# Two feed-forward blocks by seven-product block multiplication: C11 computed ahead for six pairs instead of four, and the last two products of each of their units moved behind the first two of the next unit

## The chip, the cores and the metric

The kernel runs on one core of a Trainium2 chip. The metric is the time that the device takes for one execution, in microseconds (us). An execution that the hardware profiler recorded has a time of its own, and its trace has a span, from the first to the last instruction.

A core has five engines that run side by side, each with a queue of its own that it works through in order: PE (TensorE, matrix multiplication into PSUM, with its weight loads shown as PEld), DVE (VectorE, elementwise), ACT (ScalarE, elementwise and functions), POOL (GpSimd) and SP (SyncE). Here POOL and SP mostly issue DMA transfers. An instruction that has to wait holds up everything behind it in its engine's queue.

## The reference, cut to what matters

One decoder layer over 1024 tokens of width 1024: a SwiGLU block, a mixer of two attention groups, and a second SwiGLU block. The hidden width D_FF is 2816.

```python
def _swiglu(x, g, w_gate, w_up, w_down):
    h = _rms(x, g)
    return (jax.nn.silu(h @ w_gate) * (h @ w_up)) @ w_down
...
x = x + FFN_RESID * _swiglu(x, ffn1_norm[l], ffn1_w_gate[l], ffn1_w_up[l], ffn1_w_down[l])
h = _rms(x, mix_norm[l])
...
x = x + o.astype(x.dtype) @ w_out[l]
x = x + FFN_RESID * _swiglu(x, ffn2_norm[l], ffn2_w_gate[l], ffn2_w_up[l], ffn2_w_down[l])
```

The change touches only how `h @ w_gate` and `h @ w_up` are ordered, in both blocks.

## The kernel before, in words

**Blocks and products.** `ffn` is called once for each SwiGLU block. The hidden width is 22 tiles of 128, taken as 11 pairs `c` (`NF // 2`). A pair has a gate and an up matrix, so there are 22 units, written here 0g, 0u, 1g and so on. In a unit the weights are four blocks M11, M12, M21, M22 (two hidden tiles by two halves of the features), the activations four blocks B11, B21 (first half of the tokens) and B12, B22 (second half), and the result four blocks C11, C12, C21, C22 of 128x512. The four are made with seven block products instead of eight. The operands on the weight side are M11, M12, M22 and S1 = M21 + M22, S2 = S1 - M11, S3 = M11 - M21, S4 = M12 - S2. On the activation side they are B11, B21, B22 and the sums T1 to T4.

- C11 = M11 B11 + M12 B21
- with U = M11 B11 + S2 T2: C22 = U + S3 T3 + S1 T1, C12 = U + S1 T1 + S4 B22, C21 = U + S3 T3 + M22 T4

**A product** (`product`, L357; `products`, L115) is 4 blocks of the contraction by 3 matmuls: each operand is split into a high and a low part (`split`, L99: ACT copies the high part at L101, DVE subtracts it from the source at L102), and high*high, high*low, low*high are accumulated (L122, L124, L126). So a product is 12 matmuls of 128x128 by 128x512, pinned in the order in which the program writes them. Other instructions are placed on their engines by a scheduler that follows the program's order closely.

**A unit's closing work.** `middle` (L572) takes two PSUM banks, Dk for S1 T1 and E for S3 T3, then a third, A, for S2 T2. DVE then forms `a` (U), and in two more additions C22: `a = kept + A` (L586) in the first pairs, `q = a + E` (L587), `q = q + Dk` (L588). `close` (L591) adds S4 B22 into the same bank Dk, so its first matmul must wait until L588 has read Dk. DVE forms C12 (L596). M22 T4 is added into E and DVE forms C21 (L600). `silu` (L604) runs on ACT on the gate's results, `finish` (L361) multiplies gate by up (L368, L373), stores the result to the DRAM tensor `act` and makes four more sums of it for the down projection (L385 to L388, stored at L389, L383, L390).

**The first pairs.** C11 needs only B11 and B21, so for the first FRONT = 4 pairs `front` (L394) computes M11 and M12 of two pairs at a time (16 products in all) before the rest. Meanwhile ACT and DVE make B22 and T1 to T4 from the second half of the tokens (`second_half`, L251, lines L264 to L280). The product M11 B11 is needed again in U: it is copied (L402), stored to the DRAM tensor `p1` (L404), and loaded back as `kept` (L579) in `middle`. C11 of gate times up goes to `act` through a small tile (L368, L369) and is loaded back later next to C22 (L376), and both leave with L377. All of these transfers are issued by POOL.

**The order around the change.** The list `order` (L291 to L302) gives the order in which weight operands are used. `prepare` makes them up to five products ahead, and `load_units` starts the load of a unit's raw weights (two tiles of 512 KB, L286, issued by SP) when the unit before it is made. The calls at L611 to L634 issue the products in the same order:

- pairs 0 to 3: S4 and M22 of the previous pair's up unit (`close_up`); S1, S3, S2 of g; S4, M22 of g; S1, S3, S2 of u
- pairs 4 to 10: M11, M12 of g (`start`, L558); S4, M22 of the previous up unit; S1, S3, S2 of g; M11, M12 of u; S4, M22 of g; S1, S3, S2 of u

In the first form S4 of a unit follows directly on S2 of the same unit. In the second form two products of another unit stand between them. After the pairs, `down` (L530) computes the down projection with matmuls at L518 to L520.

Of the kernel before, what the change touches and what calls it, by code (L numbers as in the profile page):

```python
# [18 lines left out]
P = 128  # L19
# [4 lines left out]
NF = DFF // P  # L24
# [22 lines left out]
CSTART = 0.5  # L47
EARLYH = 4
LEAD = 3
FRONT = 4  # L50
ESTEPS = 5
CEND = 4
MSTART = 6.5
# [8 lines left out]
def tile_layer(ctx: ExitStack, tc: tile.TileContext, x, g1n, mixn, g2n, wg1, wu1, wd1, wg2, wu2, wd2,  # L62
# [27 lines left out]
    def tmp(shape, dt=F32):  # L90
        return tpool.tile(shape, dt, tag="tmp", name=nm("tmp"))
# [131 lines left out]
    def ffn(rows_in, ys, gain, wg, wu, wd, act_d, xsrc, done, lead, aside=iter(())):  # L223
# [66 lines left out]
        PAIRS = range(NF // 2)  # L290
        order = [(c + i, m, w) for c in range(0, FRONT, 2) for w in ("M11", "M12") for i in range(2) for m in "gu"]  # L291
        for c in PAIRS:
            if c >= FRONT:
                order += [(c, "g", w) for w in ("M11", "M12")]
            if c > 0:
                order += [(c - 1, "u", w) for w in ("S4", "M22")]
            order += [(c, "g", w) for w in ("S1", "S3", "S2")]
            if c >= FRONT:
                order += [(c, "u", w) for w in ("M11", "M12")]
            order += [(c, "g", w) for w in ("S4", "M22")]  # L300
            order += [(c, "u", w) for w in ("S1", "S3", "S2")]
        order += [(NF // 2 - 1, "u", w) for w in ("S4", "M22")]  # L302
        units = [(True, c, m) for c in range(FRONT) for m in "gu"] + [(False, c, m) for c in PAIRS for m in "gu"]
        raws, sums_, ready = {}, {}, {}
# [8 lines left out]
        def make(c, nme, which):  # L313
            front = c < FRONT and which in ("M11", "M12")
            u = (front, c, nme)
            load_units(units.index(u) + (3 if front else 2))
            f1, f2 = raws[u][0], raws[u][-1]
            m = {"M11": f1[:, :512], "M12": f1[:, 512:], "M21": f2[:, :512], "M22": f2[:, 512:]}
            need = {"S1": ("M21", "M22", ALU.add), "S2": ("S1", "M11", ALU.subtract),
                    "S3": ("M11", "M21", ALU.subtract), "S4": ("M12", "S2", ALU.subtract)}  # L320
            if which in need:

                a_, b_, op = need[which]
                if which == "S1":
                    sums_["S1"] = tmp([P, 512])
                s1 = sums_["S1"]
                src = {"S1": s1, "S3": m["M21"], "S2": s1, "S4": m["M12"]}[which]
                nc.vector.tensor_tensor(src, s1 if a_ == "S1" else m[a_], s1 if b_ == "S2" else m[b_], op=op)  # L328
            else:
                src = m[which]  # L330
            s = slot([P, 2, 512], F32R)
            lows.append(split(s[:, 0, :], s[:, 1, :], src))
            ready[(c, nme, which)] = (s[:, 0, :], s[:, 1, :])
            if which == "M22" or (front and which == "M12"):
                del raws[u]
# [13 lines left out]
        def product(pt, c, nme, which, blk, first=True, ahead=AHEAD):  # L349
            assert order[used[0]] == (c, nme, which)  # L350
            prepare(ahead + 1)
            used[0] += 1
            w = ready.pop((c, nme, which))
            products(pt, [(cut(w, k * P, (k + 1) * P), blk.hi_lo(k)) for k in range(4)], first,
                     tc.keep_in_program_order)
# [3 lines left out]
        def finish(f, th, gate, up):  # L359
# [5 lines left out]
            key = "diagonal" if j == th else "other"  # L365
            if c < FRONT and j == th == 0:
                early = tmp([P, 512])
# [193 lines left out]
        def start(c, nme):  # L561

            A, Bk = ps(), ps()
            product(A, c, nme, "M11", B11)
            product(Bk, c, nme, "M12", B21)
            q = tmp([P, 512])
            nc.scalar.activation(q, A, AF.Copy)
            with behind_operands():
                nc.vector.tensor_tensor(q, q, Bk, op=ALU.add)  # L569
            return A, q  # L570

        def middle(c, nme, A):  # L572

            Dk, E = ps(), ps()
            product(Dk, c, nme, "S1", T1)
            product(E, c, nme, "S3", T3)
            if c < FRONT:
                A, kept = ps(), tmp([P, 512])
                nc.gpsimd.dma_start(kept, p1_d[c, :, "gu".index(nme), :])  # L579
            product(A, c, nme, "S2", T2, first=c < FRONT)  # L580
            a, q = tmp([P, 512]), tmp([P, 512])
            if c >= FRONT:
                nc.scalar.activation(a, A, AF.Copy)  # L583
            with behind_operands():
                if c < FRONT:
                    nc.vector.tensor_tensor(a, kept, A, op=ALU.add)  # L586
                nc.vector.tensor_tensor(q, a, E, op=ALU.add)  # L587
                nc.vector.tensor_tensor(q, q, Dk, op=ALU.add)  # L588
            return Dk, E, a, q

        def close(c, nme, Dk, E, a, between):  # L591

            product(Dk, c, nme, "S4", B22, first=False)
            q = tmp([P, 512])
            with behind_operands():
                nc.vector.tensor_tensor(q, a, Dk, op=ALU.add)  # L596
            between(q)
            product(E, c, nme, "M22", T4, first=False)
            with behind_operands():
                nc.vector.tensor_tensor(a, a, E, op=ALU.add)  # L600
            return q, a

        def silu(q):
            nc.scalar.activation(q, q, AF.Silu)  # L604

        def close_up(c, Dk, E, a, g12, g21):
            _, q = close(c, "u", Dk, E, a, lambda q: finish(2 * c, 1, g12, q))
            finish(2 * c + 1, 0, g21, q)

        late = None  # L610
        for c in PAIRS:  # L611
            if c in (4, 6):
                next(aside, None)
            A = Au = None
            if c >= FRONT:
                A, g11 = start(c, "g")
                silu(g11)
            if late:
                close_up(*late)
            Dk, E, a, g22 = middle(c, "g", A)  # L620
            silu(g22)
            if c >= FRONT:
                Au, u11 = start(c, "u")
                finish(2 * c, 0, g11, u11)
            if c == NF // 2 - 1:
                B11.t = B21.t = None
                for _ in range(2):
                    load_down(*loads.pop(0))
            g12, g21 = close(c, "g", Dk, E, a, silu)
            silu(g21)  # L630
            if c == KD - 1:
                fetch(2)
                for _ in range(PRELOAD - 2):
                    load_down(*loads.pop(0))  # L634
            Du, Eu, au, u22 = middle(c, "u", Au)
            finish(2 * c + 1, 1, g22, u22)
            late = (c, Du, Eu, au, g12, g21)
# [648 lines left out]
    order = [(h, 7 - j if h == DH + MH - 1 else j) for h in range(DH + MH) for j in range(8)]  # L1286
# [151 lines left out]
```

## Time and profile before

| | |
|---|---|
| median of 3 runs | 1913.47 us (1908.57 to 1915.0) |
| the profiled execution: its time | 1916.01 us |
| its span in the trace | 1914.2 us |
| mean granted TensorE clock of that execution | 0.983 |
| from the first down-projection matmul of the first block to its last | 474.1 to 696.1 us |
| the same in the second block | 1694.3 to 1908.9 us |

Times in the trace are counted from the span's start. A timeline row has the start, the duration, the engine, the line and operation, and in brackets how long the engine was idle before it and who ended that. A windows row has the length of a stretch, each engine's busy time with its number of instructions, the clock that TensorE was granted in the stretch (1.00 is full, 0.50 is half), the share of time that the DMA engines were busy, and GB/s. Names of buffers are `slot` (SBUF, 47 of 4 KB a partition), `tmp` (SBUF, 12 of 2 KB a partition) and `ps` (a PSUM bank, 8).

### The profile page before, as it was taken

To read this page: it belongs to the slowest core of one execution; us is meant where nothing else is said; L and a number is where in the kernel's file an instruction comes from. 1 tells how busy PE (TensorE), PEld (TensorE's weight loads), DVE (VectorE), ACT (ScalarE), POOL (GpSimd) and SP (SyncE) were. 2 spreads that over 40 slices of the span, in tenths; PEclk is the share of its full clock that TensorE was granted. 3 is DMA by queue.
4 is the path that set the end of the run, shared out by engine and by line. 5 is a ranking of instruction groups with operands and counts; after the bars stand their busy time and mean duration, and the time that the engine had idled before them with its cause. 6 is when DMAs were issued, how large, how long until landed. Compare 5 with 4: busy or idle time off the path is not lost.

```text
span 1914.2 us, 25117 instructions
## 1 busy us (share of the span) xinstructions
PE 1835.1 (96%) x9040; PEld 1548.7 (81%) x9040; DVE 1245.8 (65%) x2375; ACT 793.8 (41%) x1802; POOL 294.8 (15%) x508
## 2 busy tenths in 40 slices
PE   8888999999999999999998999997889999999998
PEld 6666888888888888889998988886678888888887
DVE  6857666665978273327888783467657665778671
ACT  7412323333445153235875672453223333334540
POOL 3011010000000022323354520211000000000000
PEclk9889999999999999999999999998999999999999
DMA  7334224324954241023311332333432332288422
GB/s 253 116 105 156 92 90 138 131 84 176 356 172 127 94 137 33 28 55 117 89 36 30 93 118 77 125 130 117 131 109 96 119 105 94 84 305 310 126 56 88
DMA packets 92326, 234.38 MB, mean 122 GB/s; under 512 B 12487, under 2 KB 18329, under 8 KB 92201
## 3 DMA queue, kind: packets, MB, share of 16 engines
q1 hardware_dynamic: 71592, 162.93, 26.3%
q0 software_dynamic: 20608, 69.85, 10.4%
q8 instruction: 71, 1.16, 0.2%
q14 instruction: 55, 0.44, 0.1%
HBM read 165.00 MB, written 63.53 MB: 119 GB/s over the span
## 4 chain that ended last, share of the span: by engine, by line
PE 85%; DVE 9%; ACT 2%; issue 2%; DMA 2%; POOL 1%; SPq 0%; DVEq 0%; ACTq 0%; POOLq 0%
PE ps L122 18%; PE ps L124 18%; PE ps L126 18%; PE ps L520 7%; PE ps L519 7%; PE ps L518 7%; DVE slot L102 2%; PE ps L847 2%; PE ps L873 1%; PE ps L821 1%; PE ps L912 1%; ACT slot L101 1%; PE ps L837 1%; PE ps L1035 1%; DMA slot<-in_wu_dram 1%
## 5 line engine op out<-in xcount | busy, mean ns | idle before, releaser
L122 PE MATMUL ps<-slot,slot 128*128 128x512 f32 (+3 forms) x1712 | 668.4, 391 | 48.7 <-DVE tmp L588 31.8
L124 PE MATMUL ps<-slot,slot 128*128 128x512 f32 (+3 forms) x1712 | 662.1, 387 | 3.6 <-DVE slot L102 3.6
L126 PE MATMUL ps<-slot,slot 128*128 128x512 f32 (+3 forms) x1712 | 661.5, 387 | 0.0
L122 PEld LDWEIGHTS ps<-slot,slot 128*128 128x128 f32 x1712 | 327.1, 191 | 118.5 <-issue 36.5
L124 PEld LDWEIGHTS ps<-slot,slot 128*128 128x128 f32 x1712 | 327.8, 191 | 66.6 <-DVE slot L102 4.4
L126 PEld LDWEIGHTS ps<-slot,slot 128*128 128x128 f32 x1712 | 326.7, 191 | 63.9
L102 DVE TENSOR_TENSOR slot<-slot,slot 128x512 fp32r<-128x512 f32 (+1 forms) x428 | 294.4, 704 | 36.1 <-ACT slot L101 33.9
L101 ACT ACTIVATE slot<-slot 128x512 fp32r<-128x512 f32 (+1 forms) x428 | 260.7, 638 | 104.3 <-PE ps L520 44.8
L101 ACT ACTIVATE slot<-tmp 128x512 fp32r<-128x512 f32 x258 | 160.5, 626 | 314.1 <-DVE tmp L328 211.0
L519 PE MATMUL ps<-slot,slot 128*128 128x512 f32 x616 | 239.8, 390 | 0.0
L520 PE MATMUL ps<-slot,slot 128*128 128x512 f32 x616 | 239.5, 389 | 0.0
L518 PE MATMUL ps<-slot,slot 128*128 128x512 f32 x616 | 237.1, 389 | 0.0
L102 DVE TENSOR_TENSOR slot<-tmp,slot 128x512 fp32r<-128x512 f32 x258 | 176.4, 687 | 21.6 <-ACT slot L101 21.3
L520 PEld LDWEIGHTS ps<-slot,slot 128*128 128x128 f32 x616 | 115.7, 188 | 24.1
L519 PEld LDWEIGHTS ps<-slot,slot 128*128 128x128 f32 x616 | 115.7, 188 | 23.9
L518 PEld LDWEIGHTS ps<-slot,slot 128*128 128x128 f32 x616 | 115.7, 188 | 23.8
L604 ACT ACTIVATE tmp<-tmp 128x512 f32<-128x512 f32 x80 | 50.6, 632 | 185.9 <-DVE tmp L596 87.5
L526 DVE SCALAR_TENSOR_TENSOR slot<-ps,slot 128x512 f32<-128x512 f32 x56 | 37.4, 688 | 81.4 <-PE ps L520 81.2
L596 DVE TENSOR_TENSOR tmp<-tmp,ps 128x512 f32<-128x512 f32 x44 | 30.3, 688 | 80.3 <-PE ps L126 79.8
L587 DVE TENSOR_TENSOR tmp<-tmp,ps 128x512 f32<-128x512 f32 x44 | 30.2, 686 | 65.4 <-ACT tmp L583 65.2
L569 DVE TENSOR_TENSOR tmp<-tmp,ps 128x512 f32<-128x512 f32 x28 | 19.3, 688 | 81.4 <-PE ps L126 81.4
L829 ACT ACTIVATE slot<-slot,tmp 128x256 f32<-128x256 f32 (+1 forms) x128 | 59.7, 468 | 27.2 <-DVE tmp L822 26.4
(180 smaller groups left out, 2033.6 us busy)
## 6 DMA issues: line engine op xcount, KB each, us to landing
tmp<-act SPq DMA_DIRECT2D x154, 256.0 KB
act<-slot POOLq DMA_DIRECT2D x58, 512.0 KB, 5.2
slot<-in_wg_dram SPq DMA_DIRECT2D x52, 512.0 KB
slot<-in_wu_dram SPq DMA_DIRECT2D x52, 512.0 KB
slot<-in_wd_dram SPq DMA_DIRECT2D x40, 512.0 KB
slot<-in_x_dram SPq DMA_DIRECT2D x16, 512.0 KB
x_mid<-slot POOLq DMA_DIRECT2D x16, 512.0 KB, 4.1
slot<-x_mid SPq DMA_DIRECT2D x16, 512.0 KB
```

What stands on the lines that cost most here:

```text
L101: nc.scalar.activation(hi, src, AF.Copy)
L102: return nc.vector.tensor_tensor(lo, src, hi.bitcast(F32), op=ALU.subtract)
L122: pin(nc.tensor.matmul(pt, ah, bh, start=first and i == 0, stop=False, skip_group_check=not first))
L124: pin(nc.tensor.matmul(pt, ah, bl, start=False, stop=False, skip_group_check=not first))
L126: pin(nc.tensor.matmul(pt, al, bh, start=False, stop=i == total - 1, skip_group_check=not first))
L518: nc.tensor.matmul(banks[i], ah, w[:, 0, :], start=first and k == 0, stop=False, skip_group_check=not first)
L519: nc.tensor.matmul(banks[i], ah, w[:, 1, :], start=False, stop=False, skip_group_check=not first)
L520: nc.tensor.matmul(banks[i], al, w[:, 0, :], start=False, stop=k == KD - 1, skip_group_check=not first)
L526: nc.vector.scalar_tensor_tensor(xv, pt, 0.5, xv, op0=ALU.mult, op1=ALU.add)
L604: nc.scalar.activation(q, q, AF.Silu)
L829: nc.scalar.activation(self.p[:, e, :w], self.p[:, e, :w], AF.Exp, bias=self.m[e], scale=-1.0, accum_out=self.den[e])
L847: nc.tensor.matmul(po[:, e * HD:(e + 1) * HD], self.pt[:, n * P:(n + 1) * P], self.head["values"](self.far, self.j, e, j - nb + 1), start= ...
```

## The change

FRONT goes from 4 to 6, so that `front` computes 24 products before the rest. For these six pairs the order of the list and of the calls is new: S1 and S3 of a unit; then S4 and M22 of the unit ahead of it (`between`, called inside `middle`); then S2 of this unit. Pairs 6 to 10 keep the second form. The sum S1 is now kept per unit (`sums_[u]`), because S1 of a unit is made while S2 and S4 of the unit ahead may still be open.

```diff
-FRONT = 4
+FRONT = 6
...
         for c in PAIRS:
-            if c >= FRONT:
-                order += [(c, "g", w) for w in ("M11", "M12")]
-            if c > 0:
-                order += [(c - 1, "u", w) for w in ("S4", "M22")]
+            if c < FRONT:
+                for m in "gu":
+                    order += [(c, m, w) for w in ("S1", "S3")]
+                    if (c, m) != (0, "g"):
+                        order += [(c, "g", w) if m == "u" else (c - 1, "u", w) for w in ("S4", "M22")]
+                    order.append((c, m, "S2"))
+                continue
+            order += [(c, "g", w) for w in ("M11", "M12")]
+            order += [(c - 1, "u", w) for w in ("S4", "M22")]
             order += [(c, "g", w) for w in ("S1", "S3", "S2")]
...
-                    sums_["S1"] = tmp([P, 512])
-                s1 = sums_["S1"]
+                    sums_[u] = tmp([P, 512])
+                s1 = sums_[u]
...
-        def middle(c, nme, A):
+        def middle(c, nme, A, between=lambda: None):
 
             Dk, E = ps(), ps()
             product(Dk, c, nme, "S1", T1)
             product(E, c, nme, "S3", T3)
+            between()
             if c < FRONT:
                 A, kept = ps(), tmp([P, 512])
                 nc.gpsimd.dma_start(kept, p1_d[c, :, "gu".index(nme), :])
...
+        def close_gate():
+            part["g12"], part["g21"] = close(*part.pop("g"), silu)
+            silu(part["g21"])
+
+        for c in range(FRONT):
+            if c in (4, 6):
+                next(aside, None)
+            Dk, E, a, g22 = middle(c, "g", None, lambda: late and close_up(*late))
+            silu(g22)
+            part["g"] = (c, "g", Dk, E, a)
+            Du, Eu, au, u22 = middle(c, "u", None, close_gate)
+            finish(2 * c + 1, 1, g22, u22)
+            late = (c, Du, Eu, au, part["g12"], part["g21"])
+
+        for c in range(FRONT, NF // 2):
...
```

The number of matmuls is the same. For pairs 4 and 5 the two `start` calls go, and with them two copies on ACT (L567, L583) and an addition on DVE (L569) in each unit. In their place come the copies to `p1`, the loads of `kept`, the addition L586 and the store and reload of C11, as in the first four pairs. In each block SP issues four more loads of 512 KB (the first half of the weights of 4g, 4u, 5g, 5u is loaded once for `front` and again for the unit).

What follows is the order on PE in the first block, where unit 0g ends its S2 product: `ps_759`, in the new kernel `ps_909`, is its bank A, and `ps_720` is its Dk. First before:

```order
L122 MATMUL ps_759<-slot_662,slot_653 128x512
L124 MATMUL ps_759<-slot_663,slot_653 128x512
L126 MATMUL ps_759<-slot_662,slot_653 128x512
L122 MATMUL ps_720<-slot_514,slot_681 128x512
L124 MATMUL ps_720<-slot_515,slot_681 128x512
L126 MATMUL ps_720<-slot_514,slot_681 128x512
```

And after the change, at the same place of the unit:

```order
L122 MATMUL ps_909<-slot_662,slot_831 128x512
L124 MATMUL ps_909<-slot_663,slot_831 128x512
L126 MATMUL ps_909<-slot_662,slot_831 128x512
L122 MATMUL ps_934<-slot_506,slot_852 128x512
L124 MATMUL ps_934<-slot_507,slot_852 128x512
L126 MATMUL ps_934<-slot_506,slot_852 128x512
```

Before, the next product after S2 writes the bank Dk of the same unit. Now a fresh bank (`ps_934`, S1 of unit 0u) is written next, and S4 into Dk of 0g follows 24 matmuls after S2.

On DVE, from the place where S2 of unit 0u has ended (L586 to L588 before are L591 to L593 in the new file, L596 is L601, L328 is L332, L373 is L377). Before, where `ps_820` is Dk:

```order
L586 TENSOR_TENSOR tmp_878<-tmp_860,ps_859 128x512
L587 TENSOR_TENSOR tmp_879<-tmp_878,ps_821 128x512
L588 TENSOR_TENSOR tmp_879<-tmp_879,ps_820 128x512
L373 TENSOR_TENSOR slot_883<-tmp_779,tmp_879 128x512
L102 TENSOR_TENSOR slot_888<-slot_722,slot_888 128x512
L596 TENSOR_TENSOR tmp_903<-tmp_878,ps_820 128x512
```

And after, where `ps_934` is Dk:

```order
L591 TENSOR_TENSOR tmp_1028<-tmp_1010,ps_1009 128x512
L592 TENSOR_TENSOR tmp_1029<-tmp_1028,ps_935 128x512
L332 TENSOR_TENSOR tmp_1043<-slot_938 128x512
L593 TENSOR_TENSOR tmp_1029<-tmp_1029,ps_934 128x512
L332 TENSOR_TENSOR slot_938<-slot_936,slot_938 128x512
L377 TENSOR_TENSOR slot_1033<-tmp_929,tmp_1029 128x512
L102 TENSOR_TENSOR slot_1045<-tmp_1043,slot_1045 128x512
L102 TENSOR_TENSOR slot_1061<-slot_938,slot_1061 128x512
L332 TENSOR_TENSOR tmp_1043<-tmp_1043,slot_936 128x512
L102 TENSOR_TENSOR slot_1077<-slot_846,slot_1077 128x512
L332 TENSOR_TENSOR slot_936<-slot_936,tmp_1043 128x512
L601 TENSOR_TENSOR tmp_1092<-tmp_1028,ps_934 128x512
```

Before, two instructions stand between the last read of Dk (L588) and the addition that waits for S4 (L596). Now seven stand there: the multiplication for C22 (L377) and six that make weight operands. One more operand sum (L332) stands ahead of the last read of Dk (L593).

On DVE ahead of the first of these additions, unit 0g's. Before (L586 is its first):

```order
L102 TENSOR_TENSOR slot_728<-tmp_726,slot_728 128x512
L586 TENSOR_TENSOR tmp_778<-tmp_760,ps_759 128x512
L102 TENSOR_TENSOR slot_744<-slot_444,slot_744 128x512
L328 TENSOR_TENSOR tmp_726<-tmp_726,slot_442 128x512
L587 TENSOR_TENSOR tmp_779<-tmp_778,ps_721 128x512
L328 TENSOR_TENSOR slot_442<-slot_442,tmp_726 128x512
L588 TENSOR_TENSOR tmp_779<-tmp_779,ps_720 128x512
L102 TENSOR_TENSOR slot_763<-tmp_726,slot_763 128x512
```

And after (L591 is its first; L372 is the product of gate and up C11 of pair 5, the last of `front`):

```order
L332 TENSOR_TENSOR tmp_850<-tmp_850,slot_680 128x512
L102 TENSOR_TENSOR slot_873<-slot_682,slot_873 128x512
L102 TENSOR_TENSOR slot_879<-slot_649,slot_879 128x512
L332 TENSOR_TENSOR slot_680<-slot_680,tmp_850 128x512
L102 TENSOR_TENSOR slot_894<-slot_651,slot_894 128x512
L372 TENSOR_TENSOR tmp_869<-tmp_867,ps_777 128x512
L102 TENSOR_TENSOR slot_913<-tmp_850,slot_913 128x512
L591 TENSOR_TENSOR tmp_928<-tmp_910,ps_909 128x512
```

Before, operand sums and splits of unit 0u stand among the three additions. Now they stand ahead of them, with the splits of S4 and M22 of 0g and with the last multiplication of `front`. Counted from the first sum of `second_half` (L264), L588 of unit 0g is DVE's 63rd instruction before. Now the last split of `second_half` is the 54th and L591 of 0g the 72nd.

More of the change, by code (lines that the diff above doesn't have):

```diff
@@ L292, in ffn @@
         for c in PAIRS:
-            if c >= FRONT:
-                order += [(c, "g", w) for w in ("M11", "M12")]
-            if c > 0:
-                order += [(c - 1, "u", w) for w in ("S4", "M22")]
+            if c < FRONT:
[7 more added lines that the diff above has]
+            order += [(c - 1, "u", w) for w in ("S4", "M22")]
             order += [(c, "g", w) for w in ("S1", "S3", "S2")]
-            if c >= FRONT:
-                order += [(c, "u", w) for w in ("M11", "M12")]
+            order += [(c, "u", w) for w in ("M11", "M12")]
             order += [(c, "g", w) for w in ("S4", "M22")]
@@ L608, in close_up @@
             finish(2 * c + 1, 0, g21, q)
-        late = None
-        for c in PAIRS:
+        late, part = None, {}
+        def close_gate():
+            part["g12"], part["g21"] = close(*part.pop("g"), silu)
+            silu(part["g21"])
+        for c in range(FRONT):
             if c in (4, 6):
                 next(aside, None)
[L614 to L619, printed above, removed]
+            Dk, E, a, g22 = middle(c, "g", None, lambda: late and close_up(*late))
[7 more added lines that the diff above has]
+                next(aside, None)
+            A, g11 = start(c, "g")
+            silu(g11)
+            close_up(*late)
             Dk, E, a, g22 = middle(c, "g", A)
             silu(g22)
-            if c >= FRONT:
-                Au, u11 = start(c, "u")
-                finish(2 * c, 0, g11, u11)
+            Au, u11 = start(c, "u")
+            finish(2 * c, 0, g11, u11)
             if c == NF // 2 - 1:
```

## The prediction

> **What bounds the kernel now.** I read the page first, then the windows, the waits of PE and the timeline of PE around each wait.
>
> ```profile
> span 1914.2 us, 25117 instructions
> PE 1835.1 (96%) x9040; PEld 1548.7 (81%) x9040; DVE 1245.8 (65%) x2375; ACT 793.8 (41%) x1802; POOL 294.8 (15%) x508
> ```
>
> PE is busy in 96% of the span, and the change leaves its 9040 matmuls as they are. So it can only bring what PE loses in gaps and in matmuls at a lower clock, and only where it reorders. I cut the windows at the first matmul of S1 of unit 0g and at the first matmul of M11 of 4g, which bound the stretch that is rewritten. By the order, 38 products of 12 stand between them, 456 matmuls.
>
> ```profile
> core 0: us, PE busy (x) PEld busy (x) DVE busy (x) ACT busy (x) POOL busy (x), PEclk, DMA share, GB/s
> 62.27:205.90 143.63, 118.43 (x457) 94.33 (x456) 91.93 (x147) 36.03 (x61) 15.25 (x26) 0.88 0.37 118
> 205.90:440.00 234.10, 234.10 (x1035) 193.06 (x1034) 155.64 (x252) 79.69 (x136) 19.80 (x29) 1.00 0.31 105
> 1289.02:1427.72 138.70, 114.92 (x458) 91.63 (x456) 92.00 (x147) 37.08 (x63) 15.24 (x26) 0.91 0.37 122
> 1427.72:1584.00 156.28, 156.28 (x691) 129.46 (x690) 104.33 (x167) 52.65 (x90) 11.40 (x17) 1.00 0.29 100
> 41.39:81.20 39.81, 30.49 (x131) 24.59 (x130) 39.81 (x67) 21.96 (x40) 4.32 (x8) 0.93 0.34 119
> 99.12:102.60 3.48, 3.48 (x9) 2.79 (x10) 1.18 (x2) 0.00 (x0) 1.07 (x2) 0.57 0.36 105
> 172.29:175.70 3.41, 3.41 (x15) 2.82 (x16) 1.55 (x3) 0.00 (x0) 1.07 (x2) 1.00 0.35 106
> ```
>
> The second and fourth rows are pairs 4 to 10, where two foreign products already stand between S2 and S4: PE has no gap and the full clock. 234.10 us over 1034 steps is 0.2264 us a matmul, 2.72 us a product. At that pace 456 matmuls take 103.2 us. The first block's stretch takes 143.63 and the second's 138.70, so 40.4 + 35.5 = 75.9 us are lost. This is the most that the change can recover there. The gaps:
>
> ```profile
> PE ps L122 <- DVE tmp L588: 31.8, 12, 3.3
> PE ps L122 <- ACT slot L101: 13.7, 2, 7.5
> PE ps L124 <- DVE slot L102: 3.6, 2, 1.8
> ```
>
> ```profile
> 69.90 0.50 PE L124 MATMUL ps<-slot,slot 128*128 128x512 f32 x1 [1.79 <-DVE slot L102]
> 80.21 0.76 PE L122 MATMUL ps<-slot,slot 128*128 128x512 f32 x1 [7.53 <-ACT slot L101]
> ...
> 96.42 0.39 PE L126 MATMUL ps<-slot,slot 128*128 128x512 f32 x1
> 99.12 0.47 PE L122 MATMUL ps<-slot,slot 128*128 128x512 f32 x1 [2.32 <-DVE tmp L588]
> ...
> 172.29 0.47 PE L122 MATMUL ps<-slot,slot 128*128 128x512 f32 x1 [2.32 <-DVE tmp L588]
> 189.51 0.76 PE L122 MATMUL ps<-slot,slot 128*128 128x512 f32 x1 [3.35 <-DVE tmp L588]
> ...
> 1296.64 0.50 PE L124 MATMUL ps<-slot,slot 128*128 128x512 f32 x1 [1.79 <-DVE slot L102]
> 1306.95 0.77 PE L122 MATMUL ps<-slot,slot 128*128 128x512 f32 x1 [6.12 <-ACT slot L101]
> ```
>
> The idle time sums to 31.8 + 13.7 + 3.6 = 49.1 us: S4 after S2 in seven units of each block, and one wait inside S2 of 0g. The other 26.8 us are matmuls at half clock behind these gaps. The row from 99.12 shows one such place, 9 matmuls in 3.48 us at a clock of 0.57, 1.4 us more than at full pace.
>
> **The change part by part.** *S4 behind two foreign products.* S4 waits because DVE must have read Dk:
>
> ```profile
> 96.84 0.69 DVE L586 TENSOR_TENSOR tmp<-tmp,ps 128x512 f32<-128x512 f32 x1 [4.81 <-PE ps L126]
> 97.56 0.69 DVE L587 TENSOR_TENSOR tmp<-tmp,ps 128x512 f32<-128x512 f32 x1
> 98.29 0.69 DVE L588 TENSOR_TENSOR tmp<-tmp,ps 128x512 f32<-128x512 f32 x1
> ```
>
> From the start of the last matmul of S2 (96.42) to the start of S4 (99.12) are 2.7 us. In the new order one operand sum stands in that chain. DVE spaces independent instructions at 39.81 / 67 = 0.594 us (row from 41.39) and dependent ones at 0.72 (97.56 less 96.84), so the chain becomes 3.3 us. The two foreign products give 0.23 + 5.43 = 5.7 us, and 2.4 us of cover are left. That is the case of an up unit, where DVE is idle before the chain.
>
> In a gate unit DVE comes later. After S4 of the up unit ahead (about 8.6 us after that unit's S2: 0.23 + 3 products + 0.2) it has fourteen instructions up to L593: C12, the sums for the down projection, operands, and the chain itself. At 0.594 plus about 0.5 for dependent pairs that ends at 17.4 us, at 0.72 each at 18.7. S4 is due after seven products, at 19.2. So 0.5 to 1.8 us of cover are left in the tightest case. Over a pair DVE has 34 instructions, 20.2 us at 0.594 and 24.5 at 0.72, against ten products, 27.2. DVE does not become the bound. I take no gap here: 14 S4 waits go.
>
> *Six pairs ahead.* Before, the first gap has another cause: DVE has no idle time from 41.39 to 81.20 and finishes `second_half` and the operands late. Now eight more products (21.7 us) come before S1 of 0g, at 84.0 instead of 62.27, and bring DVE eight splits and two multiplications (10 x 0.594 = 5.9 us). DVE gains some 16 us on PE, where the gap was 1.79 + 7.53. What is late next are the splits for pairs 4 and 5. M11 of 5u is DVE's 45th instruction from 41.39, so done at 68.1, and needed at 62.27 + 3 products + 0.5 = 70.9. M12 of 4g is the 50th, done at 71.1, needed at 73.6. At 0.69, the duration of one instruction instead of its spacing, they would be 1.5 and 2.3 us late. The row of 67 instructions is the nearest, so no gap. For S1 of 0g (56th, done at 74.7) nearly 10 us are left. The second block is built alike, with 6.12 in place of 7.53.
>
> *Clock.* Without gaps it should stay at 1.00, as it does over 234 us from 205.90 on. It does not always fall: after an equal gap of 2.32 us the row from 172.29 shows 15 matmuls at 1.00. [...] The row from 99.12 disagrees, and I go by the row: the sum over the stretches holds the clock already, and a leftover gap of 1 us may cost 2.4.
>
> *Transfers.* `kept` of a gate unit is issued on POOL behind the store that waits for C22 of the up unit ahead (L377, about 4 us after that unit's S2), and is needed when its own S2 ends, at 13.6. That leaves 9.6 us.
>
> ```profile
> 64.66 0.56 POOL L579 DMA_DIRECT2D tmp<-p  x1
> ...
> 100.53 0.54 POOL L579 DMA_DIRECT2D tmp<-p  x1
> ```
>
> ```profile
> tmp<-p POOLq DMA_DIRECT2D x16, 256.0 KB, 4.1
> toeplitz<-bias_rows POOLq DMA_DIRECT2D x2, 1024.0 KB, 10.0
> ```
>
> It lands in 4.1 us (median), so 5.5 are spare; at 10.0, the longest row, it would be 0.4 late. In an up unit it follows the last store of the pair ahead, with about as much left. Weights of 2g:
>
> ```profile
> 88.67 3.05 SPq L286 DMA_DIRECT2D slot<-in_wg_dram  x2
> ...
> 123.46 0.68 DVE L328 TENSOR_TENSOR tmp<-slot 128x512 f32<-128x512 f32 x1
> ```
>
> They are issued 34.8 us before use, 1.9 units of 143.63 / 8 = 18.0 us. With units of 13.6 us the same distance is 26 us. Some of these loads now wait for slots that stores of `act` leave; from the order I estimate 14 us to spare there. The new transfers are 5 MB a block (2 of weights, 1 + 1 to and from `p1`, 1 of C11). At 118 GB/s and a DMA share of 0.37 that is 16 us of DMA work on top of 53 (0.37 x 143.63), in 103.2 + 21.7 us: a share of 0.55. I take zero. ACT loses two copies a unit and is far from full (36.03 of 143.63).
>
> **The sum.** 1916.01 - 75.9 = 1840.1 us for the profiled execution. I leave 1.5 us for small leftovers at the tightest places, which makes 1841.6. The median of the runs shown, 1913.47, lies 2.5 below the profiled time, so the forecast is 1839.
>
> **The rivals.**
> - *Leftover gaps.* S4 of the twelve gate units in both blocks waits after all, since their cover is only 0.5 to 1.8 us. Against it stands DVE's spacing; for it, that DVE also waits for ACT's halves of the splits. With 1 us each and the clock, 12 x 2.4 = 29 us come back: 1867. Half of it gives 1853.
> - *The first gap stays.* Pairs 4 and 5 bring no relief, because their operands are as late as those of 0g were. 17.2 us (1.79 + 7.53 + 1.79 + 6.12) and about 6 of the clock remain: 1861. Against it stands the count of DVE's instructions.
> - *The clock stays low.* If the low clock were not due to the gaps, 26.8 us remain: 1864. The gapless rows at 1.00 speak against it.
> - *Slower: `kept` comes late.* DVE's chain waits for the load, and S4 behind it, in 22 units. To eat 75.9 us it takes 3.5 us a unit, that is a wait of 2.1 us and 1.4 of clock, and so a landing 11.7 us after issue, where 4.1 is the median. From there on the kernel is slower than before; at 15 us it loses 22 x (5.4 + 1.4) = 150 and stands at 1988. [...]
> - *No effect.* The gaps could move to S1 of the next unit, if no bank were free. At most seven of the eight banks are open at once by the order.
>
> **How the numbers follow.** Chances: the forecast 0.69, leftover gaps 0.15, the first gap 0.07, the clock 0.03, slower 0.05, no effect 0.01. The forecast's own range is 1832 to 1846: the runs before reach 4.9 us below their median (1908.57), and late splits at 0.69 would cost two to four us a block. Up to 1862 it takes in the first gap and the smaller half of the leftover gaps (0.07), and about 0.17 stays outside. A measurement of this kernel can tell about 0.3%, 5.7 us, from no change. Every case but the last two is faster by more: 0.94, within 0.01, slower 0.05.
>
> **What would show it right or wrong.** In the new profile the waits of PE should hold no line for L593 and none of several us for L101 or L102 early in a block, and both stretches should have a granted clock of 1.00. From S1 of 0g to the last product of pair 5 a product should take 2.72 us throughout. DVE should be idle before L591 of 0g. I am wrong if PE waits for L593 in gate units, for DVE's splits before 84 us, or for DVE behind a load of `p1`, or if the clock is low without a gap.

## The result, and the profile after

The changed kernel takes 1835.63 us (median of 4 runs, 1834.31 to 1836.06). The kernel before takes 1911.49 us (4 runs, 1908.57 to 1915.0). The ratio is 0.9601, with a 95% interval of 0.9582 to 0.9621. The forecast was 1839, with 1832 to 1846 as its own range and 1862 as the upper end with the smaller rivals. The profiled execution of the changed kernel took 1836.06 us.

The head of its page:

```profile
span 1834.3 us, 25184 instructions
PE 1807.4 (99%) x9040; PEld 1532.6 (84%) x9040; DVE 1240.9 (68%) x2375; ACT 785.9 (43%) x1794; POOL 305.8 (17%) x528
```

PE has the same 9040 matmuls and is busy in 99% of a span that is 79.9 us shorter. The windows are cut as before, at S1 of unit 0g's old place in PE's order and 456 matmuls later, in both blocks. The second row holds the same 1034 steps behind that stretch in the first block, the fourth the time in which DVE had no idle time before.

```profile
core 0: us, PE busy (x) PEld busy (x) DVE busy (x) ACT busy (x) POOL busy (x), PEclk, DMA share, GB/s
62.14:165.50 103.36, 103.36 (x457) 85.60 (x456) 80.34 (x131) 34.41 (x61) 14.33 (x25) 1.00 0.43 146
165.50:399.60 234.10, 234.10 (x1035) 193.00 (x1034) 165.36 (x269) 74.52 (x127) 26.24 (x40) 1.00 0.39 129
1244.65:1348.01 103.36, 103.36 (x458) 85.61 (x456) 80.33 (x131) 34.33 (x61) 14.33 (x25) 1.00 0.43 146
41.39:81.20 39.81, 39.81 (x178) 32.95 (x177) 38.70 (x64) 25.15 (x46) 4.87 (x9) 1.00 0.43 150
```

Where 456 matmuls took 143.63 and 138.70 us, they now take 103.36 twice, busy throughout and at a clock of 1.00: 75.6 us less. Pairs that had no gap before (second row) keep their 234.10. In the last row PE has done 47 more matmuls in the same time.

PE's waits, the first rows of that view:

```profile
engine line waited for: us in total, times, longest us
PE ps L234 <- DVE slot L198: 7.5, 2, 7.2
PE ps L178 <- DVE tmp L1222: 2.7, 3, 1.2
PE ps L1052 <- DVE tmp L1106: 2.5, 4, 1.3
```

L588 had 12 waits and 31.8 us here; its successor L593 has no row at all. Nor are there rows for the two waits of 7.53 and 6.12, or for those of 1.79 inside S2. The largest that is left, 7.5 us at L234, lies at the start of the kernel and was 7.9 before.

How much cover is left is read from DVE's end of the chain (L593) beside the start of PE's S4. DVE's rows in units 0g (the first), 1g (the next three) and 5g (the last), then PE's first matmul of S4 of 1g and of 5g, each behind the one ahead of it:

```profile
92.26 0.69 DVE L591 TENSOR_TENSOR tmp<-tmp,ps 128x512 f32<-128x512 f32 x1 [6.03 <-PE ps L126]
...
120.77 0.68 DVE L592 TENSOR_TENSOR tmp<-tmp,ps 128x512 f32<-128x512 f32 x1
121.36 0.68 DVE L332 TENSOR_TENSOR tmp<-slot 128x512 f32<-128x512 f32 x1
121.97 0.68 DVE L593 TENSOR_TENSOR tmp<-tmp,ps 128x512 f32<-128x512 f32 x1
...
232.57 0.68 DVE L593 TENSOR_TENSOR tmp<-tmp,ps 128x512 f32<-128x512 f32 x1
```

```profile
124.48 0.39 PE L126 MATMUL ps<-slot,slot 128*128 128x512 f32 x1
124.70 0.39 PE L122 MATMUL ps<-slot,slot 128*128 128x512 f32 x1
...
233.28 0.39 PE L126 MATMUL ps<-slot,slot 128*128 128x512 f32 x1
233.51 0.40 PE L122 MATMUL ps<-slot,slot 128*128 128x512 f32 x1
```

In 1g L593 ends at 122.65 and S4 starts at 124.70: 2.05 us of cover, and the same in 2g to 4g. In 0g and in the up units 0u to 4u it is 2.6. In 5g it ends at 233.25 and S4 starts at 233.51: 0.26 us. In the second block 5g has 0.15 us, and 0.14 or 0.15 us is what lay between the end of the read and the start of S4 in the kernel before, wherever S4 waited (98.98 to 99.12, for instance). So the change just fits at that place, with nothing to spare. PE pauses nowhere (0.22 or 0.23 us from the matmul ahead, its usual pace).

The loads of `kept`: in unit 1g the issue stands at 110.51, and L591 uses it at 119.57. The row of the page has the median of landing.

```profile
110.51 0.54 POOL L584 DMA_DIRECT2D tmp<-p  x1
```

```profile
tmp<-p POOLq DMA_DIRECT2D x24, 256.0 KB, 4.6
```

### The profile page after: what moved, and what is told of

It reads as the page before. It is cut to its first block, busy times and chain, and to the rows that moved or that the text cites. A ratio compares the mean times of both kernels' runs of the same rounds, so it can differ in the third digit from the quotient of the medians.

```text
span 1834.3 us, 25184 instructions
## 1 busy us (share of the span) xinstructions
PE 1807.4 (99%) x9040; PEld 1532.6 (84%) x9040; DVE 1240.9 (68%) x2375; ACT 785.9 (43%) x1794; POOL 305.8 (17%) x528
## 4 chain that ended last, share of the span: by engine, by line
PE 90%; DVE 3%; DMA 2%; ACT 2%; issue 1%; POOL 1%; SPq 0%; POOLq 0%; DVEq 0%; ACTq 0%
PE ps L122 20%; PE ps L124 20%; PE ps L126 20%; PE ps L524 7%; PE ps L523 7%; PE ps L522 7%; PE ps L864 2%; PE ps L929 1%; PE ps L890 1%; PE ps L838 1%; PE ps L854 1%; PE ps L1052 1%; DMA slot<-in_wu_dram 1%; PE ps L178 1%; ACT slot L101 1%
## 5 line engine op out<-in xcount | busy, mean ns | idle before, releaser
L122 PE MATMUL ps<-slot,slot 128*128 128x512 f32 (+3 forms) x1712 | 657.6, 385 | 3.1 <-DVE slot L218 1.6
L124 PE MATMUL ps<-slot,slot 128*128 128x512 f32 (+3 forms) x1712 | 654.0, 382 | 0.0
L126 PE MATMUL ps<-slot,slot 128*128 128x512 f32 (+3 forms) x1712 | 654.0, 382 | 0.0
L122 PEld LDWEIGHTS ps<-slot,slot 128*128 128x128 f32 x1712 | 322.0, 188 | 65.9 <-DVE slot L218 2.1
L126 PEld LDWEIGHTS ps<-slot,slot 128*128 128x128 f32 x1712 | 322.0, 188 | 61.8
L124 PEld LDWEIGHTS ps<-slot,slot 128*128 128x128 f32 x1712 | 322.2, 188 | 60.5
L101 ACT ACTIVATE slot<-slot 128x512 fp32r<-128x512 f32 (+1 forms) x428 | 259.6, 638 | 98.9 <-PE ps L524 49.0
L101 ACT ACTIVATE slot<-tmp 128x512 fp32r<-128x512 f32 x258 | 160.8, 625 | 317.0 <-DVE tmp L332 137.3
L523 PEld LDWEIGHTS ps<-slot,slot 128*128 128x128 f32 x616 | 115.7, 188 | 24.1
L524 PEld LDWEIGHTS ps<-slot,slot 128*128 128x128 f32 x616 | 115.7, 188 | 23.9
L522 PEld LDWEIGHTS ps<-slot,slot 128*128 128x128 f32 x616 | 115.7, 188 | 23.8
L136 POOL TENSOR_TENSOR small<-small,neghalf 128x1 f32<-128x1 f32 (+2 forms) x68 | 66.8, 984 | 5.0
L592 DVE TENSOR_TENSOR tmp<-tmp,ps 128x512 f32<-128x512 f32 x44 | 30.2, 686 | 51.2 <-ACT tmp L588 50.7
L864 PE MATMUL ps<-slot,slot 128*128 128x64 f32 x432 | 56.3, 269 | 2.2 <-DVE slot L856 1.6
```

Of the source, the lines that this page charges most:

```text
L101: nc.scalar.activation(hi, src, AF.Copy)
L122: pin(nc.tensor.matmul(pt, ah, bh, start=first and i == 0, stop=False, skip_group_check=not first))
L124: pin(nc.tensor.matmul(pt, ah, bl, start=False, stop=False, skip_group_check=not first))
L126: pin(nc.tensor.matmul(pt, al, bh, start=False, stop=i == total - 1, skip_group_check=not first))
L136: nc.gpsimd.tensor_tensor(r, r, neghalf[:, :w], op=ALU.pow)
L522: nc.tensor.matmul(banks[i], ah, w[:, 0, :], start=first and k == 0, stop=False, skip_group_check=not first)
```

## The experiments

Ten kernels were run, each beside the kernel before. "The two stretches" below are the 792 matmuls from the old place of S1 of 0g on, in each block: 179.64 and 179.63 us in the changed kernel, 219.87 and 214.86 in the kernel before.

**Order and lead apart.** The first has the new order with `FRONT = 4`, the second the old code with `FRONT = 6`.

Against the changed kernel, and then against the kernel before:

```diff
-FRONT = 6
+FRONT = 4
```

```diff
-FRONT = 4
+FRONT = 6
```

> The new order of products, but C11 ahead for four pairs as before. My theory: the S4 waits go, as in the changed kernel, but DVE is still behind with the second half's operands when S1 of 0g comes. By S4 of 0g about 2.4 us of operand work is added and 5.4 us of products, so of the 9.3 us of idle time early in the first block some 6 remain, and of 7.9 in the second some 5, with about 6 us of low clock: 1836 + 17 = 1853 us (1846 to 1862). Rival, pairs 4 and 5 do nothing and the order alone brings it all: 1836. Rival, the order is worth nothing without the longer lead: about 1905.

> C11 ahead for six pairs, but the old order (S4 directly behind S2). My theory: the wait of S4 belongs to the order, so it now comes in 12 units of each block, 24 in all, with 2.65 us and about 1.5 us of low clock each, 100 us; the first gap (L101, L102) is gone: 1836 + 100 = 1936 us (1920 to 1950), slower than the kernel before. Rival, the waits come from DVE being behind since the start, and the longer lead ends them: about 1860 or less.

Measured: the order alone 1850.41 us (ratio 0.9678, 0.966 to 0.9695), the lead alone 1917.07 us (1.0041, 1.0024 to 1.0057). PE's waits, first of the order alone, then of the lead alone:

```profile
PE ps L124 <- DVE slot L102: 4.8, 2, 2.4
PE ps L122 <- DVE tmp L593: 2.2, 2, 1.1
```

```profile
PE ps L122 <- DVE tmp L588: 56.6, 22, 3.4
```

The wait of S4 belongs to the order. With the old order and six pairs it comes 22 times instead of 12, and the kernel is slightly slower than before although nothing waits for the second half's operands any more. The median lies below my range (1920 to 1950); the profiled execution, at 1923.28, lies at its lower end. My figure of 24 was two too high: the last front unit has M11 and M12 of the next pair behind it already, in the old order too. And a wait cost 4.0 us with all that follows it (88.3 us more than in the changed kernel in the two stretches, over 22), where I took 4.15. The new order alone brings 60.6 of 75.4 us. The longer lead brings nothing by itself (6 us slower) and 14.8 us on top of the order, of which 11.4 lie in the two stretches (185.37 and 185.33): one gap of 2.39 and one of 1.08 in each, and one stretch at half clock each.

**The cause itself, without the new order.** If S4 waits because Dk is still to be read, it is enough to read Dk early. In the kernel before, ACT copies Dk in the first pairs right behind S1, and DVE adds to that copy. It is tried with four pairs and with six.

```diff
             product(Dk, c, nme, "S1", T1)
+            q = tmp([P, 512])
+            if c < FRONT:
+                nc.scalar.activation(q, Dk, AF.Copy)
             product(E, c, nme, "S3", T3)
...
                 if c < FRONT:
                     nc.vector.tensor_tensor(a, kept, A, op=ALU.add)
-                nc.vector.tensor_tensor(q, a, E, op=ALU.add)
-                nc.vector.tensor_tensor(q, q, Dk, op=ALU.add)
+                    nc.vector.tensor_tensor(q, q, E, op=ALU.add)
+                    nc.vector.tensor_tensor(q, q, a, op=ALU.add)
+                else:
+                    nc.vector.tensor_tensor(q, a, E, op=ALU.add)
+                    nc.vector.tensor_tensor(q, q, Dk, op=ALU.add)
```

> The kernel before with one thing changed: in the first pairs ACT copies Dk as soon as S1 has ended, and DVE adds E and U to that copy, so S4 need not wait for DVE's chain behind S2. Old order, four pairs. My theory: the 12 waits of S4 (31.8 us and some 20 us of low clock) go, the first gap stays with 17.2 us and about 6 of clock: 1859 us (1850 to 1868). Rival, S4 waits for something else that ends at about the same time (its operands, a free bank): 1905 to 1912.

> As the one before it, with C11 ahead for six pairs and still the old order. My theory: both causes are gone without any foreign product between S2 and S4, so the time is that of the changed kernel: 1836 us (1832 to 1842). Rival, the new order does more than to cover the read of Dk (it also gives DVE time for operands): 10 us or more above it, with waits of PE for L101 or L102.

Measured: 1848.32 us (0.9669, 0.9647 to 0.9692) with four pairs and 1839.39 us (0.9623, 0.9605 to 0.9641) with six. With six, both stretches run without a gap (the windows):

```profile
61.60:241.21 179.61, 179.61 (x793) 148.46 (x791) 143.13 (x228) 64.83 (x110) 25.90 (x44) 1.00 0.48 159
1248.17:1427.69 179.52, 179.52 (x794) 148.70 (x793) 143.13 (x228) 65.29 (x111) 25.90 (x44) 1.00 0.47 159
```

So the cause is shown: the read of Dk, and nothing else, held S4. The new order is one way around it, an early copy another, and in the two blocks they come out the same. The 3.8 us by which this kernel is slower than the changed one lie between the two stretches (4.1 us in the traces; the mixer, below).

The four-pair version did better than I expected, and that corrects a reading. The wait of 7.53 us in unit 0g, which I had put down to late operands, is gone in it, with the same lead of four pairs. Its waits early in a block:

```profile
PE ps L124 <- DVE slot L102: 3.6, 2, 1.8
PE ps L122 <- DVE tmp L590: 2.0, 2, 1.8
```

The second row is what is left of DVE's lag with four pairs. S1 of 0u now waits for a bank that DVE reads late, 0.20 us in the first block and 1.77 in the second: a small part of the gap has moved there.

The trace of before had the answer: S4 of 0g started at 80.21, and DVE's last read of Dk stands right ahead of it.

```profile
79.38 0.69 DVE L588 TENSOR_TENSOR tmp<-tmp,ps 128x512 f32<-128x512 f32 x1
```

It ended at 80.07. The view of waits named ACT's L101; it was L588 there too. DVE's lag at the start only made the same read 5 us later. Of 49.1 us of idle time, 45.5 were this one read.

**How large the cover is, and what a gap costs.** Into the changed kernel's chain, ahead of the last read of Dk in the gate units of the first six pairs, N instructions were put that leave the value as it is, with N = 5, 8, 2 and 3.

```diff
                 nc.vector.tensor_tensor(q, a, E, op=ALU.add)
+                for _ in range(N if c < FRONT and nme == "g" else 0):
+                    nc.vector.tensor_tensor(q, q, q, op=ALU.max)
                 nc.vector.tensor_tensor(q, q, Dk, op=ALU.add)
```

> The changed kernel with five more DVE instructions (the larger of a value and itself, so the value stays) between the second and the third addition of C22, in the gate units of the first six pairs. It measures the cover. In the trace of the changed kernel L593 of 1g ends 2.05 us before S4 of 1g starts, that of 0g 2.6. Five dependent ones at 0.72 add 3.6 us. My theory: PE waits 1.55 us in ten gate units and 1.0 in two, 17.5 us in all, and the clock stays at full speed, since by the trace of before no idle of under 1.9 us in one stretch of 3.413 us lowered it: 1836 + 17.5 = 1853 us (1846 to 1860). Rival, each such gap also lowers the clock, as half of those of 2.3 us did: 12 x 1.7 more, 1874. Rival, the cover is larger than the rows say: 1836.

> The same with eight more: 5.76 us, so gaps of 3.7 us in ten gate units and 3.2 in two, 43.5 us idle. My theory of the clock: PE's work is looked at in stretches of 3.413 us that lie on a fixed grid, and a stretch with over about 2.0 us of idle time at full clock lowers the next one to half. A gap of 3.7 us does so at nine in ten places on the grid, and costs 1.7 us, or 3.4 where a rest of the gap lies in the slow stretch: 20 to 30 us in all. 1836 + 43.5 + 25 = 1904 us (1892 to 1916). Rival, only a stretch that is wholly idle lowers the clock (a gap of 3.7 us covers one whole stretch at one place in ten): 1882.

Measured: 1932.38 us (1.0118, 1.0103 to 1.0133) and 1957.72 us (1.025, 1.0235 to 1.0266). Both expectations missed by far. The gaps were not 1.55 and 3.7 us but these (waits of PE, with five, then with eight):

```profile
PE ps L122 <- DVE tmp L595: 64.5, 12, 5.9
```

```profile
PE ps L122 <- DVE tmp L595: 90.6, 12, 8.1
```

The chain had grown by more than I put in. DVE's operand sums and splits, which stood behind it, moved in between the added instructions, eight of them. In unit 0g with five (L595 is the third addition here):

```profile
92.42 0.69 DVE L592 TENSOR_TENSOR tmp<-tmp,ps 128x512 f32<-128x512 f32 x1
...
101.57 0.69 DVE L595 TENSOR_TENSOR tmp<-tmp,ps 128x512 f32<-128x512 f32 x1
```

From the start of the one to the end of the other, at 102.26, are 9.84 us, where 1.9 us lie between them in the changed kernel. The growth is 7.95 us, in 1g too; less the cover of 2.05 that makes 5.9, and 5.88 was measured in the units 1g to 4g. The cover was read rightly, the input was not. So two more were made, with the growth counted from DVE's order:

> As the two before it, with two more instructions. Their traces showed that operand sums move in between the added ones, so the chain's growth is counted from DVE's order now: from L592 to the third addition of 1g stand 6 rows instead of 2, at 0.60 us each 2.4 us more, in 0g the same. My theory: the cover of 2.05 us leaves gaps of about 0.4 us in eight gate units (1g to 4g of both blocks), none in 0g (cover 2.6) and none in 5g (one row more); the clock stays at 1.00. Together 3 us in the two blocks, so 1836 + 3 = 1839 us, with up to 5 more where the mixer's order is another (1836 to 1846). Rival, the cover is not what the rows say: no wait of PE for L595, or several us of them in each unit.

> The same with three more: 11 rows instead of 2, 5.4 us more, so gaps of 3.4 us in eight gate units and 2.8 in two, 33 us idle. My theory of the clock (over about 2.0 us idle in one of the fixed stretches of 3.413 us lowers the next): at 8 of 10 places on the grid the clock falls, some 20 us more, with every low stretch starting on the grid: 1836 + 52 = 1888 us (1876 to 1898). Rival, only a wholly idle stretch counts: none or one of the gaps lowers the clock, 1869.

Measured: 1847.62 us (0.9665, 0.9647 to 0.9683) and 1892.3 us (0.9899, 0.9879 to 0.992). With two more, the wait in 1g:

```profile
124.92 0.39 PE L126 MATMUL ps<-slot,slot 128*128 128x512 f32 x1
125.64 0.47 PE L122 MATMUL ps<-slot,slot 128*128 128x512 f32 x1 [0.34 <-DVE tmp L595]
125.95 0.40 PE L124 MATMUL ps<-slot,slot 128*128 128x512 f32 x1
```

The gap is 0.34 us where 0.4 was expected, so the cover of 2.05 us holds. But 5g, where I expected none, has one of 1.2 in the first block and 1.3 in the second. I had taken the cover of 1g for it, and it has 0.26. The time is 1.6 above my range: the two stretches took 7.9 us more and the part between the blocks 4.5. The rows also show a price that I had left out. From 124.92 to 125.95 are 1.03 us for two steps that take 0.45 otherwise: a gap of 0.34 costs 0.58. So the restart cost about 0.24 us here beside the idle time. Two thirds of it are in how idle time is counted: from the end of the last matmul, 0.39 us after its start, where the next would have started 0.23 us after it.

With three more, the time lies in my range (1876 to 1898), and the windows show when the clock fell and when it did not. All are cut on the grid of 3.413 us on which every low stretch of this trace, that is, every stretch at half clock, begins:

```profile
128.06:131.47 3.41, 1.51 (x7) 0.93 (x5) 3.41 (x6) 2.12 (x4) 0.44 (x1) 1.00 1.01 299
131.47:134.89 3.42, 1.97 (x9) 1.68 (x10) 2.50 (x5) 0.80 (x2) 0.00 (x0) 1.00 0.67 261
134.89:138.30 3.41, 3.41 (x17) 2.83 (x16) 0.69 (x1) 0.63 (x1) 0.00 (x0) 1.00 0.00 0
1370.51:1373.92 3.41, 1.40 (x6) 1.22 (x7) 3.06 (x6) 1.26 (x2) 0.00 (x0) 1.00 0.75 294
1373.92:1377.34 3.42, 3.42 (x9) 2.66 (x9) 0.53 (x1) 0.00 (x0) 0.00 (x0) 0.50 0.00 0
```

The same gap of 3.35 us lies across two stretches at 131 us (1.90 idle in one, 1.45 in the other) and PE stays at full clock. At 1372 it puts 2.01 into one stretch, and the next runs at half. Five of the 12 gaps lowered the clock, not eight in ten: in the first block four units of 30.8 us, nearly nine stretches of the grid, followed each other, and all four gaps lay across a border.

**More lead.** The changed kernel with `FRONT = 8`.

> The changed kernel with C11 ahead for eight pairs. My theory: the stretch is at PE's pace already, so nothing more can come back, and two more pairs' copies to DRAM and back (5 MB a block) stay beside it: 1836 us (1833 to 1842). Rival, the transfers have reached what the DMA engines can do beside PE: slower by 6 us or more, with PE waiting for DVE behind a load.

Measured: 1841.25 us (0.9643, 0.9628 to 0.9657), at the upper end. The two stretches took 179.52 us each, so two pairs more of copies and loads cost PE nothing there, and bring nothing. The 5.6 us against the changed kernel lie outside: 4.3 of them between the two stretches in the traces. Part of that is the rival. In the first block, in unit 6g, which is a front unit only with eight pairs, DVE waits for the load of `kept`, and S4 waits behind DVE (the issue on POOL, the first addition, S4):

```profile
272.67 0.61 POOL L584 DMA_DIRECT2D tmp<-p  x1
283.50 0.69 DVE L591 TENSOR_TENSOR tmp<-tmp,ps 128x512 f32<-128x512 f32 x1 [3.95 <-DMA tmp<-p]
286.25 0.47 PE L122 MATMUL ps<-slot,slot 128*128 128x512 f32 x1 [2.22 <-ACT slot L101]
```

The load was issued right behind two large transfers of the mixer (`toeplitz`, L690, at 270.49) and is used 10.8 us after its issue, where 4.8 is the median. The label of the wait names L101, but L593 ended at 286.10, 0.15 us ahead of S4. In the changed kernel the last load of `kept` in this block is issued at 232.46, ahead of those transfers at 247.97. So the rival is real there. That the transfers ahead of it made the load late is read from the order, not tried. The delay of S4 is 2.4 us of the 4.3.

**The late load.** The rival on the slower side, made true: the load of `kept` is issued when S2 has ended.

```diff
-                nc.gpsimd.dma_start(kept, p1_d[c, :, "gu".index(nme), :])
             product(A, c, nme, "S2", T2, first=c < FRONT)
+            if c < FRONT:
+                nc.scalar.activation(kept[:, 0:1], A[:, 0:1], AF.Copy)
+                nc.gpsimd.dma_start(kept, p1_d[c, :, "gu".index(nme), :])
```

> The changed kernel with the load of the kept product issued only when S2 of its unit has ended (ACT writes one column of the tile from bank A first, and the load is ordered behind it). It makes the rival of the late load true: landing 4.6 us after issue, it comes some 5.5 us after S2's end, the chain ends 2.3 us later, and S4 is due 5.6 us after S2's end. My theory: PE waits some 2.5 us in each of 24 units, and the clock falls at half of them or more: 24 x (2.5 + 1.5) = 96 us, 1932 us (1905 to 1965), slower than the kernel before. Rival, the load is hidden anyway, or DVE catches up: below 1880.

Measured: 1875.69 us (0.982, 0.9803 to 0.9836). My figure is missed, and the time lies in the rival's range (below 1880), but the load is not hidden. DVE does wait for the load, and S4 behind it, in unit 0g and in 0u:

```profile
97.28 0.69 DVE L593 TENSOR_TENSOR tmp<-tmp,ps 128x512 f32<-128x512 f32 x1 [11.11 <-DMA tmp<-p]
113.73 0.69 DVE L593 TENSOR_TENSOR tmp<-tmp,ps 128x512 f32<-128x512 f32 x1 [5.64 <-DMA tmp<-p]
```

```profile
100.04 0.47 PE L122 MATMUL ps<-slot,slot 128*128 128x512 f32 x1 [2.43 <-ACT slot L101]
116.48 0.47 PE L122 MATMUL ps<-slot,slot 128*128 128x512 f32 x1 [0.97 <-ACT slot L101]
```

The load landed 3.1 us after issue (median), not 4.6, so the typical gap is 1.1 us and not 2.5. (These waits, too, are put down to ACT's L101; the last read of Dk ended at 99.89 and 116.34, 0.15 us ahead.) There are 22 gaps with 25.3 us in the two stretches, and one low stretch of the clock, behind the gap of 2.43. They took 32.8 us more: 25.3 idle, 22 x 0.24 = 5.3 for restarts, 1.7 for the clock. So the mechanism of the rival is real, and its price is lower than I put it. In 0u S2 ends at 110.08 and the chain starts 3.65 us later. Of that 2.6 are covered, and a gap costs 1.5 us in all.

## Why the prediction was right

- **The bound.** 75.9 us were lost in the two stretches, 75.6 came back. The 1.5 us that I kept for leftovers were not needed: neither stretch has a gap left.
- **S4 behind two foreign products.** In up units 2.4 us of cover were forecast and 2.6 are there (the same in 0g, where DVE is idle ahead of the chain too: L593 ends at 94.88, and S4 starts after five products of 2.72 us from 83.9). In gate units 0.5 to 1.8 were forecast. Four of the six have 2.05, since DVE's instructions were spaced at 0.60 there: another instruction stood between each addition and the one that depends on it (L591 to L593 of 1g start at 119.57, 120.77 and 121.97). 5g has 0.26, and 0.15 in the second block, below my lower end: I counted a unit in the middle and not the last one. That no gap opened there is luck. The rival of leftover gaps fell, but two more DVE instructions in the chain bring it about in five of six gate units.
- **Six pairs ahead.** The conclusion held (no wait for splits, DVE idle for 6.03 us ahead of L591 of 0g). The step "the first gap has another cause" was wrong for its larger part: it was the read of Dk again, as the early copy with four pairs shows. What the lead is worth beside the new order is 14.8 us, not 23; beside the early copy it is 8.9 (1848.32 less 1839.39).
- **Clock.** The 26.8 us that I called matmuls at half clock held some 3.8 us of restarts (16 x 0.24). The estimate that a leftover gap of 1 us may cost 2.4 was too high: with the late load 22 gaps of 1.15 us (mean) cost 1.5 each, and all but the longest left the clock alone.
- **Transfers.** `kept` has 9.06 us from issue to use, where 9.6 were forecast, and lands in 4.6. DMA's share in the stretch is 0.43, below the 0.55 that I took for harmless. The rival's break-even (a landing 11.7 us after issue) left out that 2.6 us of the chain's delay are covered, as the late load shows, so it lies later than I put it. With eight pairs one load of `kept` did come late, behind two large transfers on POOL; with six, the last load of the block is issued ahead of these.
- **What the sum did not hold.** The two profiled executions differ by 79.95 us, 4.3 more than the 75.6 of the stretches. 4.0 of that lie between the blocks' stretches, where the mixer stands, which the change does not touch. In the kernel before, one wait there is

```profile
1045.41 1.04 PE L1035 MATMUL ps<-ident,tmp 128*64 128x128 f32 x4 [2.52 <-DVE tmp L1089]
```

and in the changed kernel the same matmul does not wait:

```profile
1002.23 0.60 PE L1052 MATMUL ps<-ident,tmp 128*64 128x128 f32 x4
```

The scheduler has swapped a matmul with two transposes a little ahead of it. In ten of the twelve traces this line has a wait of 2.5 us or more, and in the two others (the changed kernel and the lead alone, both with the swap) none above 1.9. In those ten the part between the two stretches takes 2.2 to 7.2 us longer than in the changed kernel, with the lead alone 1.1 us less. It looks like a side effect of the scheduler, worth a few us; it was not tried by itself, and the ten differ in other ways too.

So the closeness of the forecast is part luck, because errors cancel. The mixer (4.3 us) and the leftovers (1.5) made the profiled execution faster than the 1841.6 of the sum. Against that, I took 2.5 us off for the distance from the profiled execution to the median, a figure of the kernel before, and in the changed kernel that distance is 0.4. The medians differ by 75.86, so close to the 75.9 of the bound, only because the profiled execution before lay 4.5 us above its median.

## What to carry to other kernels

When an accumulation goes on in a bank that another engine has to read in between, count the products that stand between the last operand of that read and the second half. Here, with none between S2 and S4, PE waited 2.3 us or more in each unit; two products of 2.72 us covered the three additions. One was not tried. Moving foreign work in between and copying the bank out early did the same, and a longer lead without either made it slightly worse (0.4%). In these runs a gap cost its idle time, about 0.24 us for the restart and, where it was longer than about 2 us, often the clock behind it (after five of the 12 gaps with three more instructions). When an edit lengthens a chain, count its length in the scheduled order, not in the source.

## What the runs showed of the hardware

**The low stretches of the clock lie on a fixed grid.** In each of these traces the low stretches of TensorE's clock are whole multiples of 3.413 us (but for one cut off by the end; in the kernel before 3.413, 6.827 and 10.240) and begin on one grid, to within 0.001 us over the whole execution. I laid that grid over PE's gaps from 62 to 280 and from 1240 to 1500 us in all twelve traces. Of 93 stretches at full clock with 0.2 to 1.9 us of idle time, 2 were followed by a stretch at half clock. Of 10 with 1.9 to 2.1 us, 7 were, and of 46 with more, all. In a stretch already at half clock the limit lay lower: up to 0.61 us idle the clock came back, from 0.63 on it stayed low. In the kernel before alone the counts are 1 of 10, 0 of 1 and 10 of 10, and at half clock it came back after 0.45 us idle and stayed low after 0.65. Both limits would fit one quantity, which is my estimate from them: the work done in a stretch, 3.41 - 2.0 = 1.4 us at full speed, (3.41 - 0.62) / 2 = 1.4 at half. It does not tell all. In both exceptions PE was busy for 1.62 us (in the kernel before from 1294.30 on, in the early copy with four pairs from 67.03 on), more than the 1.51 us that kept the clock at 128.06 above. The first of them also contradicts what I wrote ahead of the run with five more instructions, that in the kernel before no idle time of under 1.9 us in a stretch lowered the clock.

The kernel before shows the grid at the gap that ends at 99.12 and at the equal one that ends at 172.29, whose different ends I could not explain in the prediction (windows of PE alone: length, PE busy, clock, DMA share, GB/s):

```profile
96.23:99.64 3.41, 1.09 (x5) 1.00 0.00 0
99.64:103.05 3.41, 3.41 (x9) 0.50 0.46 139
...
167.91:171.32 3.41, 2.06 (x10) 1.00 0.00 0
171.32:174.73 3.41, 2.44 (x11) 1.00 0.16 56
```

The first lies in one stretch, the second across a border. So, but for the two exceptions, the clock fell after a stretch of 3.41 us that was idle for about 2.0 us or more, while the gap of 3.35 us across a border, with three more instructions, left it at 1.00.

This may also be why kernels with gaps of 2 to 3 us scatter, which is argued and not tried: 13 runs of the kernel before spread over 9.5 us and the ten of the lead alone over 11.0, while the changed kernel's four spread over 1.8. The grid does not start with the kernel (its first border lies 0.46 us after the span's start in the changed kernel, 0.65 in the kernel before, and up to 2.89 in the other traces), so the same gap can fall differently. But the numbers of runs differ, and the kernels with five and eight more instructions, whose gaps are longer, spread over 2.9 and 2.7 in four runs each.

**A wait's label can name the wrong engine.** Where S4 waited for operands and for the read of Dk at once, the view named ACT's L101 in the first block's 7.53 us, in the late-load kernel and with eight pairs. What told it was the other candidate's own row: it ended 0.14 or 0.15 us ahead of the start.
